# Where TensorE's operands lie in SBUF: activations 256 bytes off the weights' 512-byte grid, in place of 64

## The chip, the cores and the metric

The kernel runs on one core of a Trainium2 chip. The metric is the device time of one execution in microseconds (us), the median of several runs; lower is better. The engines are TensorE (PE in the profile, its weight loads PEld), VectorE (DVE), ScalarE (ACT), GpSimd (POOL) and SyncE (SP, which here only issues DMAs).

## The reference, cut to what matters

A decoder trunk of two layers works on x of 256 tokens by 1024 channels, all in float32:

```
for l in range(2):
    h = rms_norm(x, ln1)
    proj = h @ w_in                         # 1024 -> 3090 columns
    o_a = moba_mixer(...)                   # three kinds of attention on 16 heads of 64
    o_b = nsa_mixer(...)
    o_c = dilated_mixer(...)
    x = x + concat([o_a, o_b, o_c]) @ w_out            # 1024 -> 1024
    h = rms_norm(x, ln2)
    g = causal_conv3(h @ w_gate) + conv_b              # 1024 -> 2816
    x = x + (silu(g) * (h @ w_up)) @ w_down            # 2816 -> 1024
```

## The kernel before, in words

**Three matmuls for each product.** Each float32 operand of the large products is split in two float32r tiles, a high part and the rest: weights into `hi` and `lo` (lines 199 and 200: ACT copies, DVE subtracts), the normed x into `hTh` and `hTl` (lines 232 and 233), the attention's output into `oh` and `ol` (lines 539 and 540), the gated product into `aTh` and `aTl` (lines 896 and 897). `mm3` (lines 213 to 216) adds high by high, high by rest and rest by high into the same PSUM bank. In the profile the three are L214, L215 and L216.

**Stages of a layer.** `proj` multiplies by `w_in` in eight chunks of columns (`ps_in`). Here x is the operand that is loaded into the array (128 columns of `hTh` or `hTl`) and the weights are streamed past it, 256 to 512 columns at a time. The attention's steps are put between these matmuls by a table (`PUMP`). Then `down` multiplies by `w_out` (`ps_out`), `products` by `w_gate` and `w_up` (`ps_gu`, 22 blocks) and `down` again by `w_down` (`ps_dn`). In these three the weights are loaded, 128 columns of `hi` or `lo`, and 256 columns of the activation are streamed: `hTh` and `hTl`, `oh` and `ol`, `aTh` and `aTl`. So there is a new weight load for every matmul.

**Weights.** SP issues one DMA of 1 MB after the other into a ring of three `raw` tiles (the first chunk of layer 0 has a tile of its own, `raw0`). ACT and DVE split them into rings of seven `hi` and seven `lo` tiles, six parts ahead of TensorE (`weights`, lines 203 to 211). The order of the work is the order in which the program is written; the change doesn't touch it.

**Homes.** A tile's home is its byte address within each partition of SBUF. A pool's tiles are laid one behind the other in the order in which the program first asks for them, and the pools behind each other, so a tile that grows moves all that come later. The homes of the large products' operands follow from the sizes of the tiles ahead of them. Counted modulo 512 they are: every `hi` and `lo` at 0; `hTh` and `hTl` at 448, which is 64 bytes below a multiple of 512; `oh` and `ol`, `aTh` and `aTl` at 64, which is 64 bytes above one. A slice of a tile for one matmul starts 512 or 1024 bytes (or a multiple) after the tile's home, so it has the same remainder, except in the 274-column chunk. The attention's own float32r operands (`klz`, `pcz`, `vcz0`, `vcz1` at 448, `QA` and `KH` at 480) are small.

Of the kernel before, what the change touches and what calls it, by code (L numbers as in the profile page):

```python
# [11 lines left out]
F32 = mybir.dt.float32  # L12
F32R = mybir.dt.float32r
I32 = mybir.dt.int32
BF16 = mybir.dt.bfloat16
# [5 lines left out]
P = 128  # L21
S = 256
# [3 lines left out]
NM = DFF // P  # L26
# [31 lines left out]
CN = [len(c) for c in CHUNKS]  # L58
# [52 lines left out]
def emit(ctx, tc, a):  # L111
# [3 lines left out]
    cst = ctx.enter_context(tc.tile_pool(name="cst", bufs=1))  # L115
    lay = ctx.enter_context(tc.tile_pool(name="lay", bufs=2))
    wr = ctx.enter_context(tc.tile_pool(name="wr", bufs=3))
# [4 lines left out]
    def bank(tag, name):  # L122
        return pp.tile([P, 512], F32, tag=tag, name=name, bufs=BANKS[tag])
# [11 lines left out]

    klz = cst.tile([P, 2, 2, S], F32R, name="klz")
    vcz = [cst.tile([P, P], F32R, name=f"vcz{i}") for i in range(2)]
    pcz = cst.tile([P, S], F32R, name="pcz")
    for z in (vcz[0], vcz[1], pcz, klz):
        G.memset(z.bitcast(F32), 0.0)  # L140
    hTh = cst.tile([P, 8, S], F32R, name="hTh")
# [2 lines left out]
    def f(t):  # L144
        return t.bitcast(F32)
# [27 lines left out]
    splits = []  # L173
    after = []

    raw0 = wr.tile([P, 4 * 2 * CN[0]], F32, name="raw0", bufs=1)

    def fetch(u):
        if u in raws:
# [23 lines left out]
    def weights(ahead=AHEAD):  # L203
        i = taken[0]
        taken[0] += 1
        while len(ready) < min(i + 1 + ahead, len(parts)):
            with ExitStack() as st:
                for ins in after:
                    st.enter_context(tc.issue_after(ins.ins))
                split_next()  # L210
        return ready[i]

    def mm3(out, lh, ll, rh, rl, start, stop, skip=False):
        T.matmul(out, lhsT=lh, rhs=rh, start=start, stop=False, skip_group_check=skip)  # L214
        T.matmul(out, lhsT=lh, rhs=rl, start=False, stop=False, skip_group_check=skip)  # L215
        T.matmul(out, lhsT=ll, rhs=rh, start=False, stop=stop, skip_group_check=skip)  # L216

    def rsqrt(out, ss, n, tmp=None):

        v, w, q = tmp or [sml.tile(list(out.shape), F32, tag=f"rs_{i}", name=f"rs_{i}") for i in "vwq"]  # L220

        V.tensor_scalar(v, ss, 1.0 / n, EPS, ALU.mult, ALU.add)
        A.activation(out=w, in_=v, func=ACTF.Ln)
        A.activation(out=w, in_=w, func=ACTF.Exp, scale=-0.5)
        V.tensor_tensor(q, w, w, ALU.mult)
        V.scalar_tensor_tensor(q, q, -0.5, v, ALU.mult, ALU.mult)
        V.scalar_tensor_tensor(out, q, 1.5, w, ALU.add, ALU.mult)

    def make_h(k, gcol, sqs):

        g = gcol[:, k:k + 1]
        ins = [A.activation(out=hTh[:, k], in_=xT[:, k], func=ACTF.Copy, scale=g)]
        ins.append(V.scalar_tensor_tensor(out=hTl[:, k], in0=xT[:, k], scalar=g, in1=f(hTh[:, k]), op0=ALU.mult, op1=ALU.subtract))  # L233
        if sqs is not None:
            square(k, sqs)
        return ins
# [45 lines left out]
        nc.sync.dma_start(out=con[:, o0:o1], in_=a["con"][:, o0:o1])  # L282

    pools = []
    masks = cst.tile([P, 4, 384], BF16, name="masks")

    def load_masks(i):
        raw = pools[0].tile([P, 768], F32, tag="pr", name="raw_m", bufs=4)
# [31 lines left out]
    def down(acc, lT, i0, i1, last, done=None, hold=False):  # L320

        ws = [weights(0 if hold else AHEAD) for i in range(i0, i1)]
        for j in range(8):
            ps = acc[j % 4][:, (j // 4) * S:(j // 4 + 1) * S]
            js = slice(j * P, (j + 1) * P)
            for i, (hi, lo) in zip(range(i0, i1), ws):
                mm3(ps, hi[:, js], lo[:, js], lT[0][:, i], lT[1][:, i], i == 0 and j < 4, i == last, True)
            if done:
                done(j, ps)

    for L in range(DEPTH):
        sm = sms[L]
        with ExitStack() as ph:
# [519 lines left out]
            def new_x(j, ps):  # L853
                V.tensor_tensor(xT[:, j], ps, xT[:, j], ALU.add)  # L854
                after[:] = make_h(j, sm[:, O_LN2:O_LN2 + 8], sqs2)
# [2 lines left out]

        with ExitStack() as ph:
            ff = ph.enter_context(tc.tile_pool(name=f"ff{L}", bufs=2, reuse_waits="tile"))  # L860
            aTh = ff.tile([P, NM, S], F32R, tag="aTh", name="aTh", bufs=1)
            aTl = ff.tile([P, NM, S], F32R, tag="aTl", name="aTl", bufs=1)
            cw = sm[:, O_CW:O_CW + 66].rearrange("p (m w) -> p m w", w=3)
            cb = sm[:, O_CB:O_CB + 22]
            R = lay.tile([P, S], F32, tag="R", name="R", bufs=1)

            def norm2():

                ps = bank("pt", "ps_R")
                for i, sq in enumerate(sqs2):  # L870
                    T.matmul(ps[:, :S], lhsT=ones, rhs=sq, start=i == 0, stop=i == len(sqs2) - 1)
                v, w, q = [ff.tile([P, S], F32, tag=n, name="R_" + n, bufs=3) for n in ("gr", "cy", "cs")]
                rsqrt(R, ps[:, :S], D, (v, w, q))

            def products(m):
                gu = [bank((("acc", "s"), ("o", "m"))[m == 2][i], "ps_gu")[:, :S] for i in range(2)]
                ws = [weights() for _ in range(2)]
                for ps, (hi, lo) in zip(gu, ws):
                    for k in range(8):
                        cs = slice(k * P, (k + 1) * P)  # L880
                        mm3(ps, hi[:, cs], lo[:, cs], hTh[:, k], hTl[:, k], k == 0, k == 7)
                return gu

            def combine(m, g, u):
                gr = ff.tile([P, S], F32, tag="gr", name="gr", bufs=3)
                V.tensor_tensor(gr, g, R, ALU.mult)
                y = ff.tile([P, S], F32, tag="cy", name="cy", bufs=3)
                A.activation(out=y, in_=gr, func=ACTF.Identity, scale=cw[:, m, 2:3], bias=cb[:, m:m + 1])  # L888
                for j in (1, 2):
                    V.scalar_tensor_tensor(out=y[:, j:], in0=gr[:, :S - j], scalar=cw[:, m, 2 - j:3 - j], in1=y[:, j:],  # L890
                                           op0=ALU.mult, op1=ALU.add)
                s_ = ff.tile([P, S], F32, tag="cs", name="cs_", bufs=3)
                A.activation(out=s_, in_=y, func=ACTF.Silu)
                G.tensor_tensor(s_, s_, R, ALU.mult)
                V.tensor_tensor(y, u, s_, ALU.mult)  # L895
                A.copy(aTh[:, m], y)  # L896
                V.tensor_tensor(aTl[:, m], y, f(aTh[:, m]), ALU.subtract)

            waiting = []
            for m in range(NM):  # L900
                waiting.append((m, *products(m)))
                if m == 0:
                    after.clear()
                    norm2()
                if m >= 1:
                    for w in waiting:
                        combine(*w)
                    waiting = []
            acc = [bank(t, "ps_dn") for t in ("pt", "pt", "o", "m")]
            for m in range(NM - 4):  # L910
                if m == 8 and L + 1 < DEPTH:
                    tc.keep_in_program_order(A.preload_act_table_set(TABLES))
                down(acc, (aTh, aTl), m, m + 1, NM - 1)
            if L + 1 < DEPTH:
                sqs1 = []

            def new_x(j, ps):
                if L + 1 < DEPTH:
                    V.tensor_tensor(xT[:, j], ps, xT[:, j], ALU.add)
                    make_h(j, sms[L + 1][:, O_LN1:O_LN1 + 8], sqs1)  # L920
                else:
                    V.tensor_tensor(xT[:, j], ps, xT[:, j], ALU.add)
                    nc.sync.dma_start(out=a["out"][:, j], in_=xT[:, j])

            down(acc, (aTh, aTl), NM - 4, NM, NM - 1, new_x)
# [29 lines left out]
def build(arrays):  # L955
    nc = bacc.Bacc("TRN2", target_bir_lowering=False, num_devices=1, dynamic_dma_scratch_size=2048)
    a = {k: nc.dram_tensor(k, v.shape, F32, kind="ExternalInput").ap() for k, v in arrays.items()}
    a["out"] = nc.dram_tensor("out", (P, 8, S), F32, kind="ExternalOutput").ap()
    with tile.TileContext(nc) as tc, tc.manual_schedule(engines={mybir.EngineType.SP}), ExitStack() as ctx:
        emit(ctx, tc, a)  # L960
    return nc
# [7 lines left out]
```

## Time and profile before

| | |
|---|---|
| median of 3 runs | 668.0 us (665.23, 668.37, 668.0) |
| the profiled execution's own time | 668.5 us |
| its span, first to last instruction | 666.7 us |
| TensorE's granted clock, mean over the span | 0.995 of full speed |
| PE busy, matmuls | 652.1 us (98%), 5066 |
| PEld busy, weight loads | 611.3 us (92%), 5066 |
| DVE / ACT / POOL busy | 484.9 (73%) / 396.4 (59%) / 90.1 us (14%) |
| HBM traffic | 111.8 MB moved, mean 168 GB/s |

Matmuls overlap: one of 256 columns is shown as 0.28 us long, but the next one starts some 0.12 us after it started. "Busy" counts the time in which at least one runs. What a stream of matmuls costs is therefore read from the starts of its rows, not from their durations; this text calls the time from one start to the next the pitch.

### The profile page before, as it was taken

How to read it: one execution, taken by the hardware profiler on the slowest of the kernel's cores; microseconds unless marked ns; L12 is line 12 of the kernel's file. 1: busy time of each engine (PE TensorE's matmuls, PEld its weight loads, DVE VectorE, ACT ScalarE, POOL GpSimd, SP SyncE). 2: the span in 40 equal slices, each digit the busy share in tenths (PEclk: the TensorE clock that was granted, in tenths of full speed). 3: DMA queues.
4: the chain of work that ended last, by engine and by line, in shares of the span. 5: the costliest groups of instructions: out<-in, count | busy, mean ns of one | idle time of the engine just before them, and what ended most of it. 6: DMA issues, size and time to landing. Idle time of an engine off the chain costs nothing. (4 is left out here: it accounts for less than half of the span.)

```text
span 666.7 us, 12833 instructions
## 1 busy us (share of the span) xinstructions
PE 652.1 (98%) x5066; PEld 611.3 (92%) x5066; DVE 484.9 (73%) x1066; ACT 396.4 (59%) x788; POOL 90.1 (14%) x122
## 2 busy tenths in 40 slices
PE   8999999999999999999989999999999999999997
PEld 7889878789999999999988897788999999999997
DVE  6579998768877777754486899796787777776432
ACT  7467778568555555543365777876765555555320
POOL 3300000012121112100040001010312221111000
PEclk9999999999999999999989999999999999999999
DMA  8844255415555445564655422533265544456501
GB/s 323 338 144 174 64 179 183 144 65 190 180 174 176 178 180 189 190 241 147 238 185 178 136 85 82 190 127 127 77 239 190 188 174 173 176 183 240 196 1 64
DMA packets 19356, 111.84 MB, mean 168 GB/s; under 512 B 2144, under 2 KB 3936, under 8 KB 8288
## 3 DMA queue, kind: packets, MB, share of 16 engines
q1 hardware_dynamic: 19296, 111.02, 46.7%
q8 instruction: 40, 0.66, 0.4%
q14 instruction: 20, 0.16, 0.1%
HBM read 109.97 MB, written 1.05 MB: 167 GB/s over the span
## 5 line engine op out<-in xcount | busy, mean ns | idle before, releaser
L200 DVE TENSOR_TENSOR lo<-raw,hi 128x1024 fp32r<-128x1024 f32 (+3 forms) x212 | 241.7, 1149 | 75.3 <-ACT hi L199 75.0
L199 ACT ACTIVATE hi<-raw 128x1024 fp32r<-128x1024 f32 (+3 forms) x212 | 207.3, 989 | 72.2 <-PE ps_dn L215 46.6
L215 PE MATMUL ps_gu<-hTl,hi 128*128 128x256 f32 x704 | 198.0, 281 | 0.2
L214 PE MATMUL ps_gu<-hTh,hi 128*128 128x256 f32 x704 | 198.1, 281 | 0.0
L216 PE MATMUL ps_gu<-hTh,lo 128*128 128x256 f32 x704 | 197.7, 281 | 0.0
L215 PEld LDWEIGHTS ps_gu<-hTl,hi 128*128 128x128 f32 x704 | 135.0, 192 | 0.7 <-DVE hTl L233 0.6
L216 PEld LDWEIGHTS ps_gu<-hTh,lo 128*128 128x128 f32 x704 | 132.2, 188 | 0.0
L214 PEld LDWEIGHTS ps_gu<-hTh,hi 128*128 128x128 f32 x704 | 132.1, 188 | 0.1
L216 PE MATMUL ps_dn<-aTh,lo 128*128 128x256 f32 x352 | 98.6, 280 | 0.0
L215 PE MATMUL ps_dn<-aTl,hi 128*128 128x256 f32 x352 | 98.2, 279 | 0.0
L214 PE MATMUL ps_dn<-aTh,hi 128*128 128x256 f32 x352 | 98.2, 279 | 0.0
L216 PE MATMUL ps_in<-hi,hTl 128*128 128x384 f32 (+3 forms) x256 | 88.8, 348 | 2.2 <-DVE hTl L233 2.2
L214 PE MATMUL ps_in<-hi,hTh 128*128 128x384 f32 (+3 forms) x256 | 90.0, 354 | 0.8 <-ACT hi L199 0.8
L215 PE MATMUL ps_in<-lo,hTh 128*128 128x384 f32 (+3 forms) x256 | 89.3, 349 | 0.7 <-DVE lo L200 0.7
L215 PEld LDWEIGHTS ps_dn<-aTl,hi 128*128 128x128 f32 x352 | 66.2, 188 | 0.0
L216 PEld LDWEIGHTS ps_dn<-aTh,lo 128*128 128x128 f32 x352 | 66.1, 188 | 0.0
L214 PEld LDWEIGHTS ps_dn<-aTh,hi 128*128 128x128 f32 x352 | 65.8, 187 | 0.0
L896 ACT CAST aTh<-cy 128x256 fp32r<-128x256 f32 x44 | 17.9, 407 | 65.4 <-DVE cy L895 65.3
L216 PEld LDWEIGHTS ps_in<-hi,hTl 128*128 128x128 f32 x256 | 49.6, 194 | 5.6 <-DVE hTl L233 2.4
L214 PEld LDWEIGHTS ps_in<-hi,hTh 128*128 128x128 f32 x256 | 49.0, 193 | 5.7 <-issue 1.4
L215 PEld LDWEIGHTS ps_in<-lo,hTh 128*128 128x128 f32 x256 | 49.4, 193 | 4.0 <-DVE lo L200 1.1
L890 DVE SCALAR_TENSOR_TENSOR cy<-gr,sm,cy 128x255 f32<-128x255 f32 x88 | 42.1, 480 | 2.2 <-ACT cy L888 0.7
(316 smaller groups left out, 919.6 us busy)
## 6 DMA issues: line engine op xcount, KB each, us to landing
raw<-w_gu SPq DMA_DIRECT2D x44, 1024.0 KB, 4.8
raw<-w_down SPq DMA_DIRECT2D x22, 1024.0 KB, 4.6
raw<-w_in SPq DMA_DIRECT2D x16, 768.0 KB, 4.2
raw<-w_in SPq DMA_DIRECT2D x8, 1024.0 KB, 4.6
raw<-w_out SPq DMA_DIRECT2D x8, 1024.0 KB, 4.8
w<-cw SPq DMA_DIRECT2D x4, 1024.0 KB, 10.9
raw<-w_in SPq DMA_DIRECT2D x4, 512.0 KB, 3.7
raw<-w_in SPq DMA_DIRECT2D x4, 274.0 KB, 5.3
```

The lines of the kernel that those rows point to most:

```text
L199: splits[:] = [A.activation(out=hi[:, :n], in_=r, func=ACTF.Copy), V.tensor_tensor(out=lo[:, :n], in0=r, in1=f(hi[:, :n]), op=ALU.subtract)]
L200: V.tensor_tensor(out=lo[:, :n], in0=r, in1=f(hi[:, :n]), op=ALU.subtract)]
L214: T.matmul(out, lhsT=lh, rhs=rh, start=start, stop=False, skip_group_check=skip)
L215: T.matmul(out, lhsT=lh, rhs=rl, start=False, stop=False, skip_group_check=skip)
L216: T.matmul(out, lhsT=ll, rhs=rh, start=False, stop=stop, skip_group_check=skip)
L890: V.scalar_tensor_tensor(out=y[:, j:], in0=gr[:, :S - j], scalar=cw[:, m, 2 - j:3 - j], in1=y[:, j:], op0=ALU.mult, op1=ALU.add)
L896: A.copy(aTh[:, m], y)
```

## The change

Four tiles are asked for with more room than they use, and the use is cut back to a slice of the old shape. No instruction is added, removed or moved.

```diff
-    pcz = cst.tile([P, S], F32R, name="pcz")
+    pcz = cst.tile([P, S + 80], F32R, name="pcz")[:, :S]
...
-    raw0 = wr.tile([P, 4 * 2 * CN[0]], F32, name="raw0", bufs=1)
+    raw0 = wr.tile([P, 4 * 2 * CN[0] + 80], F32, name="raw0", bufs=1)
...
-    masks = cst.tile([P, 4, 384], BF16, name="masks")
+    masks = cst.tile([P, 4 * 384 + 192], BF16, name="masks")[:, :4 * 384].rearrange("p (a b) -> p a b", a=4)
...
-            aTh = ff.tile([P, NM, S], F32R, tag="aTh", name="aTh", bufs=1)
+            aTh = ff.tile([P, 48 + NM * S], F32R, tag="aTh", name="aTh", bufs=1)[:, 48:].rearrange("p (m s) -> p m s", m=NM)
```

What this does to the homes, worked out from the sizes (80 float32 are 320 bytes, 192 bfloat16 are 384, 48 float32 are 192):

| tiles | moved by, bytes | modulo 512 before | after |
|---|---|---|---|
| `hTh`, `hTl` | 320 | 448 (-64) | 256 |
| `oh`, `ol` | 320 + 384 = 704 | 64 | 256 |
| `raw` ring, `hi`, `lo` | 704 + 320 = 1024 | 0 | 0 |
| `aTh`, `aTl` | 1024 + 192 = 1216 | 64 | 256 |
| `klz`, `vcz0`, `vcz1`, `pcz` | 0 | 448 | 448 |
| `QA`, `KH` and the rest of the attention's pool | 1024 | 480 and others | the same |

## Rows read from the trace of the kernel before

**Rows 1.** The page, part 1: busy time, share, instructions of each engine.

```profile
PE 652.1 (98%) x5066; PEld 611.3 (92%) x5066; DVE 484.9 (73%) x1066; ACT 396.4 (59%) x788; POOL 90.1 (14%) x122
```

**Rows 2.** Groups by line, shapes apart, PE alone; idle time stands last.

```profile
L214 PE MATMUL ps_gu<-hTh,hi 128*128 128x256 f32 x704 | 198.1, 281 | 0.0
...
L214 PE MATMUL ps_dn<-aTh,hi 128*128 128x256 f32 x352 | 98.2, 279 | 0.0
...
L214 PE MATMUL ps_out<-oh,hi 128*128 128x256 f32 x128 | 36.1, 288 | 0.2 <-ACT ksv L389 0.2
...
L214 PE MATMUL ps_in<-hi,hTh 128*128 128x256 f32 x32 | 9.5, 296 | 0.0
```

**Rows 3.** Busy time by stretch: PE, PEld, DVE, ACT, POOL; clock, DMA share, GB/s.

```profile
160.00:260.00 100.00, 100.00 (x851) 100.00 (x851) 77.48 (x126) 58.18 (x91) 19.01 (x18) 1.00 0.52 185
...
153.00:155.00 2.00, 2.00 (x20) 2.00 (x19) 2.00 (x3) 2.00 (x3) 0.00 (x0) 1.00 0.00 0
640.00:660.00 20.00, 20.00 (x173) 20.00 (x172) 4.69 (x8) 2.12 (x2) 0.00 (x0) 1.00 0.08 28
```

**Rows 4.** Timeline of PE in `ps_gu`, layer 0: start, duration in us.

```profile
199.74 0.28 PE L214 MATMUL ps_gu<-hTh,hi 128*128 128x256 f32 x1
...
204.93 0.28 PE L216 MATMUL ps_gu<-hTh,lo 128*128 128x256 f32 x1
```

**Rows 5.** The same in `ps_dn` at the end of layer 1.

```profile
656.80 0.28 PE L214 MATMUL ps_dn<-aTh,hi 128*128 128x256 f32 x1
...
662.92 0.28 PE L215 MATMUL ps_dn<-aTl,hi 128*128 128x256 f32 x1
```

**Rows 6.** The same in the 256-column chunk of `ps_in`, layer 0.

```profile
108.80 0.28 PE L215 MATMUL ps_in<-lo,hTh 128*128 128x256 f32 x1
...
109.98 0.28 PE L216 MATMUL ps_in<-hi,hTl 128*128 128x256 f32 x1
```

**Rows 7.** The same in the second half of `ps_gu`'s first block, layer 0.

```profile
152.88 0.28 PE L215 MATMUL ps_gu<-hTl,hi 128*128 128x256 f32 x1
...
155.03 0.28 PE L216 MATMUL ps_gu<-hTh,lo 128*128 128x256 f32 x1
155.15 0.59 PE L871 MATMUL ps_R<-sqs,ones 128*128 128x256 f32 x2
155.39 0.47 PE L214 MATMUL ps_gu<-hTh,hi 128*128 128x256 f32 x1
155.69 0.28 PE L215 MATMUL ps_gu<-hTl,hi 128*128 128x256 f32 x1
```

**Rows 8.** The same in `ps_out`, layer 1.

```profile
460.41 0.28 PE L214 MATMUL ps_out<-oh,hi 128*128 128x256 f32 x1
...
460.98 0.28 PE L216 MATMUL ps_out<-oh,lo 128*128 128x256 f32 x1
```

**Rows 9.** Timeline of PEld at a restart: two loads in a row.

```profile
152.07 0.19 PEld L215 LDWEIGHTS ps_gu<-hTl,hi 128*128 128x128 f32 x1 [0.30 <-DVE hTl L233]
152.18 0.19 PEld L216 LDWEIGHTS ps_gu<-hTh,lo 128*128 128x128 f32 x1
```

**Rows 10.** Weight loads by line in `ps_gu` (160 to 260 us).

```profile
L215 PEld LDWEIGHTS ps_gu<-hTl,hi 128*128 128x128 f32 x284 | 54.5, 192 | 0.0
L216 PEld LDWEIGHTS ps_gu<-hTh,lo 128*128 128x128 f32 x284 | 53.3, 188 | 0.0
```

**Rows 11.** Weight loads by line in `ps_dn` (277 to 327 us).

```profile
L215 PEld LDWEIGHTS ps_dn<-aTl,hi 128*128 128x128 f32 x142 | 26.7, 188 | 0.0
```

## The prediction

> **What bounds the kernel now.** I read the page's busy times first: TensorE has a matmul running in 98% of the span, DVE is busy 73% of it, ACT 59% [rows 1]. The groups by line with shapes kept apart say where: the matmuls that stream 256 columns of float32r are 3 x 704 in `ps_gu`, 3 x 352 in `ps_dn`, 3 x 128 in `ps_out` and 3 x 32 in one chunk of `ps_in`, 3648 in all, and before them TensorE idled for next to nothing [rows 2]. The busy times by stretch then show that nobody holds TensorE up there: in `ps_gu` DVE is busy 77% and ACT 58% of the time at the full granted clock, with the DMA engines half used [rows 3]. So the span is the sum of the pitches (start to start) of these matmuls, plus the broken-up attention stages, and an edit of homes can act only through the pitch.
>
> The timeline gives the pitch. In `ps_gu` 44 steps take 204.93 - 199.74 = 5.19 us [rows 4], in `ps_dn` 52 steps take 662.92 - 656.80 = 6.12 us [rows 5]: together 11.31 us for 96 steps, 117.8 ns. In `ps_in`, where the roles are exchanged (activation loaded, weight streamed), 10 steps take 1.18 us, 118 ns [rows 6]. But there is a second pitch: in the second half of `ps_gu`'s first block 19 steps take 155.03 - 152.88 = 2.15 us, 113.2 ns [rows 7], and in `ps_out` 5 steps take 0.57 us, 114 ns [rows 8]. The tiles and homes in the stretches with the short pitch are those of the stretches with the long one beside them. The short pitch of `ps_gu` ends at an interruption (the two matmuls of L871), behind which the same loop goes on at the long pitch [rows 7].
>
> **The change part by part.** It adds no instruction, wait or DMA; the order on every engine and queue stays. What it removes and adds are homes only, so there are three things to price.
>
> *The homes of the streamed activations against the loaded weights* (and the reverse in `ps_in`), from 64 bytes below (`hTh`, `hTl`) or above (the others) to 256. The two ends: if every one of the 3648 took the short pitch, 3648 x (117.8 - 113.2 = 4.6 ns) = 16.8 us less; if each got as much slower, 16.8 us more. The chunks with 274, 384 and 512 columns are left out of both; no long stretch of them shows two clean pitches. I take zero, for three reasons from the rows. First, -64 in `ps_gu`, +64 in `ps_dn` and exchanged roles in `ps_in` give the same 118 ns within the rounding of the starts [rows 4 to 6]: a shift of 128 bytes changes nothing, and a dependence that is blind to 128 bytes but sees 192 (from 64 to 256) would be an odd one. Second, the short and the long pitch both exist at unchanged homes, at -64 [rows 4, 7] as well as at +64 [rows 5, 8]. What chooses is how the stream restarts after an interruption, thus timing. Third, two loads in a row start 0.11 us apart [rows 9], so a load takes about as long as the stream of a matmul. In that time the load crosses 512 bytes of each partition and the stream 1024. My estimate from this: the distance between the two reading places grows by some 512 bytes within every matmul, so whatever remainder modulo 512 it starts from, it passes through all of them once.
>
> Against zero stands one trace of an effect: in `ps_gu` the load of L215 takes 192 ns, that of L216 188 [rows 10]; in `ps_dn` L215 has 188 too [rows 11]. So the side on which the activation lies shows in one of three loads, by 4 ns, while the pitch doesn't show it. This keeps both ends alive.
>
> The Trainium skill ("SBUF — State Buffer", section "Who interferes with whom") says that TensorE has two independent read ports, one for the moving operand and one for weight loads, and that "PE and ACT never wait on anyone". By that rule the homes cannot matter and the sum is zero; the trace agrees in that the pitch is the long one while DVE and DMA rest, and the short one while DVE and ACT are both fully busy [rows 3], but the rule has no room for two pitches of the same instruction.
>
> *The homes that DVE, ACT and POOL write and read* (the two activation pairs, `masks`, and all that lies behind). Their cost lies beside TensorE, which has been the later one throughout [rows 1, 3]; the slack in `ps_gu` is 23 us of each 100 on DVE. If that cover were gone, a tenth on DVE's 77 us per 100 would still fit into it. Zero.
>
> *The attention's own operands* keep their remainder modulo 512: zero.
>
> The sum is 0 on the profiled execution's own 668.5 us (span 666.7 and 1.8 around it), which lies 0.5 us over the median of the runs shown. The streams restart after the same interruptions, so I expect the same pitches; where a redraw falls otherwise it can only gain, since the four longest streams have the long pitch now. Half a microsecond under the median: **667.5 us**, its own range 664 to 671.
>
> **The rivals.**
>
> *Full effect: the short pitch becomes the rule.* Place: all four kinds of streams. It would hold if the long pitch came from the loads and the stream meeting in one part of SBUF, a part larger than 128 bytes, and 256 keeps them apart. For it: the two pitches are there, the difference isn't due to other engines [rows 3], and it has the right size to be contention of a load with a stream. Against it: the three reasons above. Time: 668.5 - 16.8 = 651.7, so about 652 us. DVE would then have some 77/96 of the time in `ps_gu`, no new bound.
>
> *Part of it.* Only `ps_gu` (3 x 704 x 4.6 ns = 9.7 us, 659 us) or only the three kinds with +64 (1536 x 4.6 = 7.1 us, 661 us), because one of the sides was the bad one; or no effect of the homes but another restart: one of the two `ps_gu` streams of some 1000 matmuls behind L871 falling into the short pitch gives 4.6 us, 664 us. One of the two `ps_dn` streams of some 500 gives 2.4 us, which lies in the range of no change.
>
> *The other side: the load is held up.* Place: the weight loads in `ps_gu`, `ps_dn` and `ps_out`. At 256 the load meets the stream in each of three matmuls and not in one: the load is then 4 ns longer, as L215's is now [rows 10], and this time it does decide, since load and stream are about equally long [rows 9]. Price: one matmul in three 4.6 ns later makes 5.6 us (674 us), all of them 16.8 us (685 us); I would say 676. It decides as soon as the load ends behind the stream. For it: the 192 ns; against it: a load that is 4 ns longer costs nothing now.
>
> **How the numbers follow.** No change has 0.47, the full effect 0.20, part of it 0.16, slower 0.17. A measurement of this kernel can tell about 0.5% (3.3 us) from no change, so no change reaches from 664.7 to 671.3, and the chances are: faster 0.36, same 0.47, slower 0.17. The range must reach down to the full effect, which is too likely to be left out, so to 651; at the top it goes to 672 and leaves out nearly all of the slower case and a little below: 651 to 672.
>
> **What would show it.** Right: the timeline has 117.8 ns in the long streams of `ps_gu` and `ps_dn`, in both layers, and 113 only in short pieces after an interruption; PE's share stays 98%. The full effect: 113 ns from the first matmul behind L871 to the end of `ps_dn`, and a `ps_gu` stage (22 blocks of 48 matmuls) shorter by 1056 x 4.6 ns = 4.9 us per layer. The slower one: loads of 192 ns or more on all three lines and a pitch over 118. What would make the prediction wrong is a dependence of the pitch on the homes that is the same at -64, +64 and in exchanged roles, and another at 256. My weakest step is the second reason: that the pitch follows from the restart doesn't exclude that at 256 one of the two cannot last.

## The result, and the profile after

The changed kernel takes 673.2 us (672.32 to 674.22, 4 runs) against 666.69 us (665.23 to 668.37) for the kernel before beside it: a ratio of 1.0102, 95% interval 1.0078 to 1.0126, so 6.5 us more. The forecast was no change, 667.5 us, range 651 to 672: the kernel became slower, and the time lies above the range. The profiled execution took 672.32 us, its span is 670.4 us.

The page's busy times, for [rows 1]: TensorE still has a matmul running 98% of the span, only longer; the other engines do what they did.

```profile
PE 657.5 (98%) x5066; PEld 616.9 (92%) x5066; DVE 484.8 (72%) x1066; ACT 396.8 (59%) x788; POOL 90.2 (13%) x122
```

Busy time by stretch of the changed kernel, for [rows 3]: in the 100 us of `ps_gu` there are 836 matmuls in place of 851, at the full clock and with the same work on DVE and ACT; in the quiet 20 us of `ps_dn` 169 in place of 173.

```profile
160.00:260.00 100.00, 100.00 (x836) 100.00 (x835) 77.55 (x126) 58.68 (x92) 19.02 (x18) 1.00 0.51 181
640.00:660.00 20.00, 20.00 (x169) 20.00 (x168) 5.12 (x7) 3.17 (x3) 0.00 (x0) 1.00 0.04 12
```

PE's timeline in `ps_gu` of layer 0, in `ps_dn` of layer 1, in the 256-column chunk of `ps_in`, and in the second half of the first `ps_gu` block, for [rows 4 to 7]. L216 to L218 are the three lines of `mm3` after the change.

```profile
199.72 0.28 PE L216 MATMUL ps_gu<-hTh,hi 128*128 128x256 f32 x1
...
204.88 0.28 PE L217 MATMUL ps_gu<-hTl,hi 128*128 128x256 f32 x1
...
656.80 0.28 PE L216 MATMUL ps_dn<-aTh,hi 128*128 128x256 f32 x1
...
662.92 0.28 PE L216 MATMUL ps_dn<-aTh,hi 128*128 128x256 f32 x1
...
107.73 0.28 PE L218 MATMUL ps_in<-hi,hTl 128*128 128x256 f32 x1
...
109.53 0.28 PE L218 MATMUL ps_in<-hi,hTl 128*128 128x256 f32 x1
...
150.82 0.28 PE L217 MATMUL ps_gu<-hTl,hi 128*128 128x256 f32 x1
...
153.22 0.28 PE L216 MATMUL ps_gu<-hTh,hi 128*128 128x256 f32 x1
```

The steps between each two rows are 43, 51, 15 and 20, so the pitches are 5.16/43, 6.12/51, 1.80/15 and 2.40/20 us: 120.0 ns in every one, where there were 117.8, 117.8, 118 and 113.2. The short pitch is gone even from the place where the kernel before had it. The weight loads by line (160 to 260 us), for [rows 10], show the other half: now each of the three takes 192 ns, in `ps_dn` too (the last row, 280 to 327 us, for [rows 11]).

```profile
L218 PEld LDWEIGHTS ps_gu<-hTh,lo 128*128 128x128 f32 x279 | 53.6, 192 | 0.0
L216 PEld LDWEIGHTS ps_gu<-hTh,hi 128*128 128x128 f32 x278 | 53.4, 192 | 0.0
L217 PEld LDWEIGHTS ps_gu<-hTl,hi 128*128 128x128 f32 x278 | 53.4, 192 | 0.0
...
L217 PEld LDWEIGHTS ps_dn<-aTl,hi 128*128 128x128 f32 x131 | 25.2, 192 | 0.0
```

The sum: 3648 matmuls x 2.2 ns = 8.0 us. The starts bear it out: from its first to its last matmul `ps_gu` takes 127.3 and 127.2 us in the two layers in place of 125.0, and `ps_dn` 63.2 in place of 62.1; over both layers that is 6.9 us for these 3168 matmuls, 2.2 ns each.

The two profiled spans differ by only 3.7 us. The one of before had low-clock stretches that the one of after had not: in 335 to 357 us the granted clock was 0.92 before and 1.00 after (below, one row of each kernel). There TensorE had waited 2.2 us for `hTl` before the change and started its 274-column matmuls 0.23 us apart behind that; after the change it had waited 1.6 us, and they start 0.13 us apart. Over its span the mean clock was 0.995 against 1.000, and at 1.2 in place of 2.4 GHz that lack costs an estimated 0.005 x 666.7 = 3.3 us. 8.0 - 3.3 = 4.7; 1.0 us of the difference of the profiles is not assigned. The median of the runs differs by 6.5. Among the runs with a mean clock of 1.000, the difference is 7.6 us: 672.9 on average for three of the changed kernel (672.32 to 673.53) against 665.3 for seven of the kernel before (663.82 to 666.23, all run beside experiments 1 to 10).

```profile
335.00:357.00 22.00, 19.80 (x122) 19.04 (x122) 17.23 (x25) 15.08 (x27) 6.48 (x10) 0.92 0.63 213
```

```profile
335.00:357.00 22.00, 20.40 (x138) 19.64 (x137) 17.28 (x25) 15.89 (x30) 7.72 (x13) 1.00 0.63 213
```

### The profile page after: what moved, and what is told of

The parts are those of the page before. It is cut to its first block, busy times and chain, and to the rows that moved or that the text cites. A ratio compares the mean times of both kernels' runs of the same rounds, so it can differ in the third digit from the quotient of the medians.

```text
span 670.4 us, 12833 instructions
## 1 busy us (share of the span) xinstructions
PE 657.5 (98%) x5066; PEld 616.9 (92%) x5066; DVE 484.8 (72%) x1066; ACT 396.8 (59%) x788; POOL 90.2 (13%) x122
## 5 line engine op out<-in xcount | busy, mean ns | idle before, releaser
L216 PE MATMUL ps_gu<-hTh,hi 128*128 128x256 f32 x704 | 199.6, 283 | 0.0
L218 PE MATMUL ps_gu<-hTh,lo 128*128 128x256 f32 x704 | 199.2, 283 | 0.0
L216 PEld LDWEIGHTS ps_gu<-hTh,hi 128*128 128x128 f32 x704 | 135.1, 192 | 0.1
L218 PEld LDWEIGHTS ps_gu<-hTh,lo 128*128 128x128 f32 x704 | 135.1, 192 | 0.0
L216 PE MATMUL ps_dn<-aTh,hi 128*128 128x256 f32 x352 | 99.6, 283 | 0.0
L217 PE MATMUL ps_dn<-aTl,hi 128*128 128x256 f32 x352 | 99.6, 283 | 0.0
L218 PE MATMUL ps_dn<-aTh,lo 128*128 128x256 f32 x352 | 99.6, 283 | 0.0
L216 PE MATMUL ps_in<-hi,hTh 128*128 128x384 f32 (+3 forms) x256 | 88.8, 350 | 0.3 <-ACT hi L201 0.3
L218 PE MATMUL ps_in<-hi,hTl 128*128 128x384 f32 (+3 forms) x256 | 87.6, 343 | 1.6 <-DVE hTl L235 1.6
L217 PE MATMUL ps_in<-lo,hTh 128*128 128x384 f32 (+3 forms) x256 | 87.9, 344 | 0.6 <-DVE lo L202 0.6
L216 PEld LDWEIGHTS ps_dn<-aTh,hi 128*128 128x128 f32 x352 | 67.6, 192 | 0.0
L218 PEld LDWEIGHTS ps_dn<-aTh,lo 128*128 128x128 f32 x352 | 67.6, 192 | 0.0
L218 PEld LDWEIGHTS ps_in<-hi,hTl 128*128 128x128 f32 x256 | 48.3, 189 | 5.0 <-DVE hTl L235 1.8
L216 PEld LDWEIGHTS ps_in<-hi,hTh 128*128 128x128 f32 x256 | 48.0, 189 | 5.2 <-issue 1.4
```

## The experiments

Two questions: do the homes make the pitch, and if so, what is the rule? The offset is always the activation's home less the weights' (at 0), modulo 512 or 256 bytes. Each map below is one run, with operands that are all zero.

**1. A map of offsets.** A kernel with nothing but streams, in this loop:

```
for d in range(0, 128, 4):                  # float32 columns: 16 bytes a step
    for r in range(3):                      # three kinds of interruption
        ...
        for k in range(8):
            T.matmul(ps[:, :S], lhsT=W[:, 0, ks], rhs=X[:, 0, xs], ...)   # hi, h
            T.matmul(ps[:, :S], lhsT=W[:, 0, ks], rhs=X[:, 1, xs], ...)   # hi, l
            T.matmul(ps[:, :S], lhsT=W[:, 1, ks], rhs=X[:, 0, xs], ...)   # lo, h
```

> This kernel computes nothing of the reference: it only runs streams of 24 float32r matmuls (128 columns loaded, 256 streamed, in mm3's order hi/h, hi/l, lo/h) with the weights at 0 modulo 512 and the activation at 0, 16, 32, ... 496, three streams for each offset, each begun behind another kind of interruption (two float32 matmuls of 256 columns; one of 128; one of 1 column). No other engine works meanwhile. Theory 1 (the pitch follows from where the load and the stream read, modulo 512): the pitch is a function of the offset: 117.8 ns (or 113.3) at 64 and at 448, 120.0 at 256 whatever the interruption, and some offsets hold 113.3 to the end of a stream. Theory 2 (what chooses the pitch is the timing of the restart, or a part of the change other than the distance of the homes, such as the ring's shift by 1024 bytes): the offsets don't differ; for the same interruption all 32 have one pitch, or the pitches are scattered with no order in the offset.

Measured: mean pitch of the last 12 steps of a stream, ns, worked out from the starts in the trace; three interruptions for each offset. The very first stream still began with matmuls 213 ns apart (128.5).

```
offset  0: 128.5 120.0 120.0   16: 118.4 118.7 118.8   32: 116.7 116.7 116.7   48: 118.3 118.3 118.3
       64: 117.8 117.8 117.8   80: 120.0 120.1 120.0   96: 120.1 120.0 120.0  112: 113.3 114.8 113.3
      128: 119.9 118.8 118.2  144: 119.1 118.6 118.5  160: 117.0 118.6 119.0  176: 119.4 119.4 119.4
      192: 113.2 113.3 113.3  208: 119.1 118.5 118.8  224: 118.2 118.3 118.4  240: 117.2 117.2 116.8
      256: 120.0 120.1 120.1  320: 117.8 117.9 117.8  368: 113.3 114.8 113.4  448: 113.4 113.3 113.3
```

The same in the timeline, streams at 256 (18 steps) and at 448 (19 steps): 2.16/18 = 120.0 and 2.15/19 = 113.2 ns, on a core where DVE, ACT and DMA rest. Starts are shown to 0.01 us, so a pitch from the rows of 11 steps is good to about 1 ns, and from 45 steps to about 0.2; the tables are from unrounded starts.

```profile
176.19 0.28 PE L147 MATMUL dayw<-X,W 128*128 128x256 f32 x1
...
178.35 0.28 PE L147 MATMUL dayw<-X,W 128*128 128x256 f32 x1
...
293.76 0.28 PE L146 MATMUL dmyw<-X,W 128*128 128x256 f32 x1
...
295.91 0.28 PE L147 MATMUL dmyw<-X,W 128*128 128x256 f32 x1
```

So the homes change the pitch with nothing else at work. It repeats after 256 bytes (but for one of three streams at 16 against 272, and the very first stream), and 256 is the same as 0, where load and stream start alike: among the worst of this map. The weights stay at 0 in the map, so it can't tell the distance from the activation's own address. `ps_in` can: its streamed tile, the weights, stays at 0 in both kernels, only the loaded activation moved from 448 to 256, and the pitch went from 118 [rows 6] to 120.0 ns. So the streamed tile's address alone doesn't decide. By the distance, stream less load, it is 64 and then 0 modulo 256, where the map has 117.8 and 120.0. At 448 all three entries gave 113.3, though `ps_gu` before stands at 448 and has 117.8 in its long streams: this the offset alone doesn't explain.

**2. One part undone.** The changed kernel without the pad of `aTh`, so `aTh` and `aTl` are back at 64 while the ring keeps its new place:

```diff
-            aTh = ff.tile([P, 48 + NM * S], ...)[:, 48:].rearrange("p (m s) -> p m s", m=NM)
+            aTh = ff.tile([P, NM, S], F32R, tag="aTh", name="aTh", bufs=1)
```

> The changed kernel with the pad of aTh undone: aTh and aTl back at 64 modulo 512, everything else (hTh, hTl, oh, ol at 256, the ring moved by 1024 bytes) as changed. Theory 1 (distance of the homes): ps_dn goes back to 117.8 ns a matmul while ps_gu stays at 120.0; 1056 x 2.2 ns = 2.3 us less than the changed kernel, about 671 us, ratio to before 1.006. Theory 2 (the ring's move, or timing): ps_dn stays at 120.0 and the time at 673.

673.45 us, ratio to before 1.0113 (1.0086 to 1.0139): the time alone doesn't tell 671 from 673. (The one run here with a mean clock of 1.000 took 670.33 us, against 672.32 to 673.53 for the changed kernel's three; the other runs here had 0.992 to 0.994.) The timeline does, `ps_gu` then `ps_dn`, 43 steps each: 120.0 and 117.7 ns. `ps_dn` is back, with the ring still moved, so the ring's move is not the cause. The move is a multiple of 512 bytes and leaves the distance modulo 512 as it was.

```profile
199.74 0.28 PE L217 MATMUL ps_gu<-hTl,hi 128*128 128x256 f32 x1
...
204.90 0.28 PE L218 MATMUL ps_gu<-hTh,lo 128*128 128x256 f32 x1
...
289.82 0.28 PE L217 MATMUL ps_dn<-aTl,hi 128*128 128x256 f32 x1
...
294.88 0.28 PE L218 MATMUL ps_dn<-aTh,lo 128*128 128x256 f32 x1
```

**3. Separate offsets and entries.** The streams of experiment 1 with `X[:, 0]` (h) at `dh` and `X[:, 1]` (l) at `dl`, 81 pairs, each entered in four ways.

> Computes nothing of the reference; only streams of 24 float32r matmuls, no other engine at work. Now the high and the rest part of the activation get separate offsets from the weights, each out of 0, 32, 64, 96, 112, 128, 160, 192, 224 bytes, 81 pairs, and each pair is entered in four ways: without a break from a stream at 64 or at 0, behind two float32 matmuls of 256 columns, and behind four of 64 by 128 columns. Theory A (offsets alone decide, each load against the stream beside it): a pair's pitch is 2/3 of the way the high part's own and 1/3 the rest's (equal offsets gave 113.3 at 192, 117.8 at 64, 120.0 at 0), and the entry doesn't matter: 192 stays at 113.3 even when it is entered from a stream at 64. Theory B (at some offsets both pitches can last, and the entry chooses): the pair 192, 192 has 113.3 for some entries and 117.8 for others, as ps_gu has in the kernel before; then other pairs should be found that have 113.3 for all four.

Theory A fell: none of the 72 unequal pairs went below 116.7 ns, however good each offset was alone (high part at 112, rest at 192: 118.9 to 120.1). On the diagonal, entered from 64, from 0, behind two matmuls, behind four:

```
 0: 120.0 120.0 120.0 120.0     64: 117.8 117.8 113.3 117.8    112: 113.3 113.3 114.8 113.3
32: 116.7 117.8 116.7 116.7     96: 120.0 120.0 120.0 120.0    192: 117.8 113.3 113.3 117.8
```

That is theory B: at 192 and at 64 two pitches can last (over streams of 24 matmuls) and the entry chooses; at 0 and 96 all four entries end at 120.0; at 112 nearly all end at 113.3. What in the entry chooses stays open: at 64, two float32 matmuls ahead gave 113.3 here and in experiment 6, and 117.8 in experiments 1 and 11.

**4. and 5. The whole kernel with all activations at 448, and at 192.** Pads changed (`pcz` 0 or 64 columns, `aTh` 96 or 32, `raw0` to bring the ring back to 0).

> The whole kernel with hTh, hTl (where they were before) and now also oh, ol, aTh, aTl at 448 modulo 512, which is 192 modulo 256, where the map has 113.3 ns. Theory A: ps_dn and ps_out take 113.3 ns, ps_gu stays as before (its homes are those of before); 1440 x 4.5 ns = 6.4 us less than before, 660 us, ratio 0.990. Theory B (entry decides): ps_dn follows ps_gu without a break and inherits its 117.8 ns; time as before, 666 us.

> The same with all activations at 192 modulo 512. If only the remainder modulo 256 counts, the same as with all at 448, state for state: 660 us by theory A, 666 us by theory B. If 192 and 448 differ in the kernel, as the map says they don't, ps_gu at 113.3 ns too: 3648 x 4.5 ns = 16 us less, 650 us.

661.82 us (ratio 0.9924, 0.9895 to 0.9953) and 661.78 us (0.9934, 0.9907 to 0.9961). The two agree, and both theories missed the inside: `ps_gu`, whose homes modulo 256 had not changed, went to the short pitch and `ps_dn` did not (`ps_out` did, in its unbroken stretches, as theory A had it). With all at 192, 46 and 44 steps:

```profile
199.76 0.28 PE L216 MATMUL ps_gu<-hTh,hi 128*128 128x256 f32 x1
...
204.97 0.28 PE L217 MATMUL ps_gu<-hTl,hi 128*128 128x256 f32 x1
...
289.78 0.28 PE L216 MATMUL ps_dn<-aTh,hi 128*128 128x256 f32 x1
...
294.96 0.28 PE L218 MATMUL ps_dn<-aTh,lo 128*128 128x256 f32 x1
```

5.21/46 = 113.3 and 5.18/44 = 117.7 ns. After 646 steps at 113.3 the stream breaks up into blocks of 48 that begin with a gap and then have one pitch or the other; the last one enters `ps_dn` at 117.8, and that lasts, in both layers. That `ps_dn` takes over the pitch that it is entered with is what B says; why `ps_gu` now begins with the short one is not shown.

**6. A fine map**, steps of 4 bytes, four entries.

> Computes nothing of the reference; streams of 24 float32r matmuls only, the activation's high and rest part at one offset from the weights, from 0 to 252 bytes in steps of 4, each entered in the four ways of the map of pairs. If the pitch comes from where load and stream read (theory A with the states of theory B on top), it is smooth over a few neighbouring steps, and there is a small window about 112 with 113.3 for all four entries; at 64 and 192 113.3 for some and 117.8 for others; 120.0 for all at 0. If instead 16-byte or 64-byte lines decide, the steps inside a line give one value and it changes only at multiples of 16 or 64.

Not smooth, and not constant within 16 bytes: 100 to 128 gave (first entry) 120.6, 120.0, 120.0, **113.3**, 121.7, 122.2, 120.0, 118.8. Of these 64 offsets only 64, 112 and 192 showed 113.3 at all (in the first map one stream at 272 did), and only 112 for all but one entry (114.8). A model for this I don't have.

**7. The whole kernel with all six activation tiles at 112 modulo 256**, each a slice of a tile with 64 columns more:

```diff
-    hTh = cst.tile([P, 8, S], F32R, name="hTh")
+    hTh = cst.tile([P, 64 + 8 * S], F32R, name="hTh")[:, 44:44 + 8 * S].rearrange("p (k s) -> p k s", k=8)
...
+    # hTl alike; oh, ol, aTh, aTl with [:, 12:12 + ...]
```

> The kernel before with all six activation tiles at 112 modulo 256, where every entry of the maps led to about 113.3 ns. Theory (offset and entry, as in the maps): 113.3 ns in ps_gu, ps_dn and ps_out in all stretches, also behind an interruption; against before 2112 x 4.4 ns in ps_gu, less some 6 us in which the PSUM banks of ps_gu come free too late (as with all at 192), 1056 x 4.4 ns in ps_dn and some 1 us in ps_out: 9.3 - 6 + 4.7 + 1 = 9 us less, 657 us, ratio 0.987. Rival (writes of the other engines to SBUF also choose, so that a map without them does not carry over): ps_gu at 117.8 or 120, the time as before or slower, 666 us.

659.67 us, ratio 0.9903 (0.9873 to 0.9933). `ps_gu` and `ps_dn`, 45 steps each, have 113.6 and 113.3 ns; the map without the other engines carries over, the rival falls.

```profile
199.82 0.28 PE L215 MATMUL ps_gu<-hTl,hi 128*128 128x256 f32 x1
...
204.93 0.28 PE L215 MATMUL ps_gu<-hTl,hi 128*128 128x256 f32 x1
...
289.81 0.28 PE L215 MATMUL ps_dn<-aTl,hi 128*128 128x256 f32 x1
...
294.91 0.28 PE L215 MATMUL ps_dn<-aTl,hi 128*128 128x256 f32 x1
```

But the last third of `ps_gu` gave part of the gain back. PEld's timeline (two starts of a block) and DVE's in the same kernel: from 230 us on each block waits for DVE's y, which waits for POOL, and the blocks follow each other 241.31 - 235.54 = 5.77 us apart. At 113.3 ns 48 matmuls take 5.44 us, at 117.8 they took 5.65, so here the new wait costs more than the pitch brings.

```profile
235.54 0.19 PEld L214 LDWEIGHTS ps_gu<-hTh,hi 128*128 128x128 f32 x1 [0.21 <-DVE cy L895]
241.31 0.19 PEld L214 LDWEIGHTS ps_gu<-hTh,hi 128*128 128x128 f32 x1 [0.21 <-DVE cy L895]
...
240.83 0.42 DVE L895 TENSOR_TENSOR cy<-ps_gu,cs__3006 128x256 f32<-128x256 f32 x1 [0.63 <-POOL cs__3006 L894]
```

**8. to 10. The chain shortened, with and without the homes.**

```diff
-                G.tensor_tensor(s_, s_, R, ALU.mult)
+                V.tensor_tensor(s_, s_, R, ALU.mult)          # 8: on all at 112; 9: on the kernel before
...
-                V.tensor_tensor(y, u, s_, ALU.mult)           # 10, on all at 112:
+                V.tensor_tensor(w, u, R, ALU.mult)            #   right behind gr
+                G.tensor_tensor(y, w, s_, ALU.mult)           #   in place of L894 and L895
```

> All activations at 112 modulo 256, and the multiplication of silu by R (L894) on DVE in place of POOL. With all at 112 the first 13 blocks of ps_gu run at 113.4 ns and the later ones (7.5 per layer) each lose some 0.33 us (5.77 us from block to block, 48 x 113.3 ns = 5.44). Theory: what holds them is the chain from the end of a block through gr, the conv, silu, POOL's 1.12 us and DVE's y to the freed PSUM bank; with 0.42 us on DVE in place of POOL's 1.12 and two hand-overs it is some 0.7 us shorter, the later blocks take 5.44 us too, and the kernel 2 x 7.5 x 0.33 = 5 us less than all at 112: 655 us, ratio to before 0.983. Rival: DVE itself (4.95 us busy of each 5.44 then) or the order of the weight splits holds the blocks; then 659 us or more.

> The kernel before with only that multiplication moved to DVE, homes as before. ps_gu has no gaps at 117.8 ns, so both theories expect no change, 666 us within 0.5%; it shows whether the gain of the run beside it needs the homes.

> All at 112; the same chain shortened in another way: DVE multiplies u by R as soon as a block is done, which frees the PSUM bank, and POOL multiplies the product by silu, behind it. By the theory the bank is free at once and the later blocks take 5.44 us: 655 us. By the rival (DVE's order: it now waits for POOL and ACT before the rest of the product) 659 us or more.

Measured, against 665.61 us of before beside them: 8: **654.24 us** (0.9823, 0.9798 to 0.9849); 9: 666.45 (1.0002, 0.9978 to 1.0026); 10: 654.96 (0.9834, 0.9805 to 0.9862). Both ways to shorten the chain give the 5 us, the first does nothing without the homes (the second was not tried there), and DVE did not become the bound, although in experiment 8 it is busy 58.40 of 65 us in `ps_gu`:

```profile
160.00:225.00 65.00, 65.00 (x576) 65.00 (x575) 58.40 (x103) 41.72 (x65) 0.00 (x0) 1.00 0.59 199
225.00:270.00 45.00, 45.00 (x399) 45.00 (x399) 39.33 (x68) 26.86 (x42) 0.00 (x0) 1.00 0.56 190
```

Experiments 8 and 10 beat both kernels; 8 is 11 us under the kernel before and some 19 under the changed one.

Experiment 9 brought something else. Its homes are those of before, and its profiled execution (662.32 us; its ten runs go from 662.22 to 668.72) has `ps_gu` at the short pitch in layer 0 (46 steps, 5.22 us, 113.5 ns) and at the long one in layer 1 (44 steps, 5.18 us, 117.7 ns):

```profile
199.74 0.28 PE L215 MATMUL ps_gu<-hTl,hi 128*128 128x256 f32 x1
...
204.96 0.28 PE L216 MATMUL ps_gu<-hTh,lo 128*128 128x256 f32 x1
...
529.75 0.28 PE L214 MATMUL ps_gu<-hTh,hi 128*128 128x256 f32 x1
...
534.93 0.28 PE L216 MATMUL ps_gu<-hTh,lo 128*128 128x256 f32 x1
```

So at 448 one program's two layers can differ with the same homes: 1007 steps x 4.4 ns = 4.4 us. That is about the spread of the runs of the kernels at 448; that the spread comes from it is an inference from one profile.

The weight loads of these two layers also set a reading of [rows 10] right. At the same home L215's load takes 188 ns in layer 0, with the short pitch, and 192 in layer 1, with the long one (160 to 260 and 490 to 590 us):

```profile
L215 PEld LDWEIGHTS ps_gu<-hTl,hi 128*128 128x128 f32 x295 | 55.4, 188 | 0.0
...
L215 PEld LDWEIGHTS ps_gu<-hTl,hi 128*128 128x128 f32 x284 | 54.5, 192 | 0.0
```

**11. Other shapes.** The streams at offsets 0 to 240 with 64 columns loaded, and with 384 and 512 streamed.

> Computes nothing of the reference; streams of 24 float32r matmuls only, at offsets 0, 16, ... 240, each behind two float32 matmuls, in four shapes: 128 columns loaded and 256 streamed (as in the maps before), 64 loaded and 256 streamed, 128 and 384, 128 and 512. Theory (a load that runs as long as the stream is delayed by it, and then decides when the next matmul starts): with 64 columns the load ends long before the stream, so the pitch is one value for all offsets and not above 113.3 ns; with 384 and 512 columns the offsets matter little, within 2 to 3 ns about 173 and 229. Rival (the stream itself is held up where it meets the load, whatever ends last): with 64 columns the offsets still differ, by about half as much; with 384 and 512 by as many ns as with 256, 113 to 120 becoming some 167 to 174 and 220 to 231.

```
            0     16    32    48    64    80    96    112   128   144   160   176   192   208   224   240
128 x 256  119.5 118.5 116.7 118.2 117.8 119.9 119.9 113.3 118.8 118.9 118.5 119.4 113.2 119.5 118.3 117.4
 64 x 256  113.3 116.7 118.7 118.3 116.7 117.6 116.8 116.7 116.7 113.3 117.1 115.9 119.3 116.7 116.6 113.3
128 x 384  173.3 175.5 176.7 175.0 173.2 174.9 176.7 173.2 175.7 174.7 173.2 175.8 176.6 176.8 173.3 180.0
128 x 512  226.8 231.7 233.3 233.3 228.9 231.1 233.3 231.1 233.3 233.3 234.3 233.4 233.4 234.8 233.4 236.8
```

My theory fell: a load of 64 columns, whose row is 134 ns long in place of 188 (11 steps each, at offset 0 and at 192: 1.24/11 = 112.7 and 1.31/11 = 119.1 ns in the timeline), leaves differences about as large, with other good offsets. So the offsets matter also where the load ends early. The rival had that, but not the size (no half for half the load); that the stream itself is held up where it meets the load is what it assumes, and no row shows it. With one stream for each value, what the entry does here isn't known.

```profile
35.00 0.28 PE L140 MATMUL dazv<-X,W 128*64 128x256 f32 x1
...
36.24 0.28 PE L139 MATMUL dazv<-X,W 128*64 128x256 f32 x1
...
261.33 0.28 PE L140 MATMUL dmzv<-X,W 128*64 128x256 f32 x1
...
262.64 0.28 PE L139 MATMUL dmzv<-X,W 128*64 128x256 f32 x1
```

## Why the prediction was wrong

**The step that failed** is the term of the sum that was put at zero, the homes of the streamed activations against the loaded weights. It is 2.2 ns for each of the 3648 matmuls: 8.0 us by the sum, 7.6 between the runs at full clock, 6.5 between the medians. Of the three reasons for the zero, two fail and one is half of the truth.

**What held.** The kernel is the sum of its pitches, and none of the other terms put at zero shows in the result. The homes that the other engines use cost nothing (DVE 484.9 and 484.8 us busy). The slower case had the right place and sign: the loads of all three lines at 192 ns, a pitch over 118, as its part of "what would show it" said; its price, taken from the step between the two pitches seen (4.6 ns for one or all of three), was too high, 674 to 685 where 673.2 came. Its mechanism, a load that ends behind the stream, is not shown, and experiment 11 speaks against it. It was given 0.17, and the range was cut just below it.

**The first reason failed.** "A shift of 128 bytes changes nothing" was read from -64, +64 and exchanged roles, which all had 118 ns. The map shows why: -64 is 192 modulo 256, and at 64 and at 192 a pitch of 117.8 happens to be able to last. It is a coincidence of two offsets, not blindness: 0 and 128, or 112 and 240, also lie 128 apart and differ by some 1 to 4 ns. Two equal points were taken for a flat line.

**The second reason was half of the truth.** That something besides the homes chooses between the pitches was shown by experiments 3, 4 and 9. But the choice is among those that the offset allows, and at 256 (as at 0) only some 120 ns was seen, whatever the entry. The prediction named this as its weakest step and gave it too little.

**The third reason failed.** That load and stream pass through all distances, so that the start doesn't matter, would make the map flat; it has steps of 8 ns between offsets 4 bytes apart.

**The 192 ns were misread.** The prediction took L215's longer load for a mark of the side on which the activation lies that "costs nothing now". In experiment 9 it comes and goes at one home, together with the pitch: 192 ns with 117.8, 188 with 113.3. It was a mark of the long pitch at 448. (At 64 the long pitch has loads of 188 ns [rows 11], so it is no general one.)

**The rule.** The Trainium skill ("SBUF — State Buffer", section "Who interferes with whom") has TensorE's two read ports independent and TensorE waiting for no one. The maps contradict the first for float32r: with all other engines idle, the same matmuls take 113.3 to 124.5 ns, depending on where the load's and the stream's operands lie to each other and, at some offsets, on the entry. The measurement decides. That nobody else is waited for agrees: map and kernel have the same pitches, 113.3, 117.8 and 120.0 ns.

**The full effect, a rival at 652 us**, exists, at 112 and not at 256, and it came to 659.67 us first: "no new bound" on DVE was right, but the chain through POOL was one.

What stays open: why a remainder modulo 256 bytes, in steps as fine as 4, makes these pitches, why no unequal offsets of the two parts came below 116.7 ns, and what in an entry chooses. The runs show the map and not the mechanism.

## What to carry to other kernels

When a matmul stream is the bound, read its pitch from the starts and look for two values of the same instruction: a gap between them is time that no engine's row explains. Where the loaded and the streamed operand lie to each other can be that gap, and its map is jagged, so measure it with a kernel of bare streams at the very shapes, entered in several ways, before padding anything; a few points that agree prove nothing about the next one. When the stream then gets shorter, look at once for the chain that was hidden by 4%.

## What the runs showed of the hardware that was not expected

For float32r, 128 columns loaded and 256 streamed, the pitch depends on the distance of the operands in the partition, modulo 256 bytes: 113.3 ns at 112, 120.0 at 0, up to 124.5 at 132. In the long streams of the kernels the values are 113.33, 117.78 and 120.00 ns, each the same to 0.1 ns in every stage that has it; at 2.4 GHz these are 816, 848 and 864 cycles for three matmuls, apart by multiples of 16. At some offsets two of them can last, and which one it is then holds for a thousand matmuls; as far as the runs show, what went before chooses.
